# Strassen's seven products for the up-projections of two feed-forward layers

## The chip, the core and the metric

One core of a Trainium2 chip runs the whole program. The metric is the device time of one execution in microseconds (us). The engines named here are TensorE (PE: matmuls, with its weight loads as PEld), VectorE (DVE), ScalarE (ACT) and SyncE (SP, which issues DMAs). PSUM has eight banks of 512 float32 columns on 128 partitions; a matmul writes into one of them.

## What is computed

Two transformer blocks, one after the other, on one sequence of 1024 tokens with 1024 channels, all in float32: a mixer (state space, Fourier and attention branches in the first block; a gated recurrence and its neighbours in the second), then a feed-forward layer (FFN), each with norms and a residual. The FFNs are what the change is about:

```
up = dwconv3(h @ w_up, conv_w, conv_b)          # FFN 1, w_up: 1024 x 2*2816, width-3 convolution over tokens
gate, val = split(up, 2)
y = (gelu(gate) * val) @ w_down                 # w_down: 2816 x 1024

hid = square(relu(u @ w_up))                    # FFN 2, w_up: 1024 x 4096
m = hid @ w_down                                # w_down: 4096 x 1024
```

## The kernel before

Every float32 product is made of three passes: an operand x is split into `hi`, its cast to a shorter type (ScalarE), and `lo = x - hi` (VectorE), and the product is hi·hi + lo·hi + hi·lo (`mm3`, L144 to L156; `split`, L171). A weight block is 128 x 1024; `Weights._prep` (L121) loads it (512 KB, SP queue), casts it (L130) and subtracts (L131), one block ahead of its use. There are three buffers each for `whi` and `wlo`.

The up-projection puts hidden channels on the output's partitions: a block of 128 hidden channels is 8 channel steps x 3 passes x 2 halves of the tokens = 48 matmuls of 512 columns into two banks (`lin`, L159). FFN 1 makes a gate block and a value block (`ps_g`, `ps_v`; L418 on), convolves each out of PSUM (`conv`, L401: one ScalarE instruction, L406, and two VectorE instructions, L409 and L410), applies gelu (L427), multiplies (L429) and splits the result into `ghi` and `glo`. FFN 2 makes one block, relu on ScalarE (L449), its square on VectorE (L450), and splits it. FFN 1 has 22 such steps, FFN 2 has 32. The first blocks after a boundary are made by parts of the tokens (`halves`, L371), since the activations (`acth`, `actl`) come in by parts.

The down-projection puts tokens on the partitions: `rows_group` (L347) takes two hidden blocks, and for each of eight row tiles runs 2 x 3 x 2 matmuls into `ps_row` and adds the result to Y in SBUF (`rows_sum`, L329, VectorE L335; the first group is copied by ScalarE, L333). `ffn` (L384) goes by groups of two hidden blocks: up-projection of group G, then down-projection of group G - 1; the last group takes four blocks and runs beside the boundary (norm, residual, transposes, next activations). So up- and down-projection alternate through the whole FFN, and the hidden blocks stay in SBUF.

Each engine works through its instructions in a fixed order, which a scheduler lays down when the program is built.

## Time and profile before

| | |
|---|---|
| median of 3 runs | 2741.04 us (2740.24 to 2744.2) |
| span of the profiled execution, first to last instruction | 2737.2 us |
| PE busy | 2675.8 us (98%), 12572 matmul records |
| PEld busy | 2195.7 us (80%) |
| VectorE busy | 1449.3 us (53%) |
| ScalarE busy | 885.0 us (32%) |
| mean granted TensorE clock | 0.995 of 2.4 GHz |

The time of a run lies some 4 us above the span. Mixer 1 takes 0 to 455, FFN 1 480 to 1147, the boundary behind it to 1215, mixer 2 to 2020, FFN 2 2055 to 2695, and the rest is its last group and the output. Matmuls overlap in their records (0.39 us each, one started every 0.23 us), so the pace of PE is read from starts.

### The profile page before, as it was taken

What the parts mean: (1) busy time and instruction counts of PE and PEld (TensorE: products, weight loads), DVE (VectorE), ACT (ScalarE), POOL (GpSimd) and SP (SyncE); (2) the same over time, 40 slices, a digit from 0 to 9 for tenths busy, and PEclk for the clock granted to TensorE, in tenths of its full rate; (3) what the DMA queues carried; (4) which work ended last, traced back from release to release, by engine and by line L of the source; (5) the groups of instructions that cost most, each with busy time, mean ns of one, the idle gap of its engine ahead of it and who ended that gap; (6) DMA issues with size and microseconds to landing.
All of it is one profiled execution on the core that took longest, in us unless ns stands there. A gap on an engine that the chain in (4) does not pass through costs nothing.

```text
span 2737.2 us, 30502 instructions
## 1 busy us (share of the span) xinstructions
PE 2675.8 (98%) x12572; PEld 2195.7 (80%) x12572; DVE 1449.3 (53%) x2428; ACT 885.0 (32%) x1335; POOL 0.2 (0%) x4
## 2 busy tenths in 40 slices
...
GB/s 257 86 71 146 164 57 179 54 47 46 54 47 46 47 47 46 71 130 39 39 39 34 54 45 40 54 46 54 77 155 56 52 47 47 47 54 39 58 51 108
DMA packets 65484, 193.62 MB, mean 71 GB/s; under 512 B 10305, under 2 KB 19905, under 8 KB 65346
## 3 DMA queue, kind: packets, MB, share of 16 engines
...
## 4 chain that ended last, share of the span: by engine, by line
PE 88%; DVE 7%; ACT 2%; DMA 1%; issue 1%; SPq 0%; ACTq 0%; DVEq 0%
PE ps_row L322 8%; PE ps_row L324 8%; PE ps_row L326 8%; PE ps_z L154 7%; PE ps_z L156 7%; PE ps_z L152 7%; PE ps_u L152 4%; PE ps_u L156 4%; PE ps_u L154 4%; PE ps_g L152 3%; PE ps_v L152 3%; PE ps_g L154 3%; PE ps_v L154 3%; PE ps_g L156 3%; PE ps_v L156 3%; PE ps_bo L152 1%
## 5 line engine op out<-in xcount | busy, mean ns | idle before, releaser
L131 DVE TENSOR_TENSOR wlo<-wraw,whi 128x1024 fp32r<-128x1024 f32 x208 | 254.3, 1223 | 871.7 <-ACT whi L130 871.5
L130 ACT CAST whi<-wraw 128x1024 fp32r<-128x1024 f32 x208 | 218.8, 1053 | 1219.3 <-PE ps_row L326 330.4
L335 DVE TENSOR_TENSOR y<-y,ps_row 128x512 f32<-128x512 f32 x398 | 256.2, 681 | 151.1 <-PE ps_row L326 151.1
L152 PE MATMUL ps_z<-acth,whi 128*128 128x512 f32 x960 | 302.3, 396 | 0.2 <-ACT z L1046 0.2
L154 PE MATMUL ps_z<-actl,whi 128*128 128x512 f32 x960 | 300.1, 392 | 1.9 <-DVE actl L173 1.9
L156 PE MATMUL ps_z<-acth,wlo 128*128 128x512 f32 x960 | 298.1, 391 | 0.0
L324 PE MATMUL ps_row<-wlo,ghi 128*128 128x512 f32 x792 | 245.4, 389 | 0.0
L322 PE MATMUL ps_row<-whi,ghi 128*128 128x512 f32 x792 | 245.3, 389 | 0.0
L326 PE MATMUL ps_row<-whi,glo 128*128 128x512 f32 x792 | 244.1, 389 | 0.0
L154 PEld LDWEIGHTS ps_z<-actl,whi 128*128 128x128 f32 x960 | 179.9, 188 | 40.2 <-DVE actl L173 2.4
L156 PEld LDWEIGHTS ps_z<-acth,wlo 128*128 128x128 f32 x960 | 179.9, 188 | 37.3 <-issue 0.2
L152 PEld LDWEIGHTS ps_z<-acth,whi 128*128 128x128 f32 x960 | 178.4, 188 | 39.0 <-issue 1.7
L322 PEld LDWEIGHTS ps_row<-whi,ghi 128*128 128x128 f32 x792 | 148.7, 188 | 31.1
L326 PEld LDWEIGHTS ps_row<-whi,glo 128*128 128x128 f32 x792 | 148.7, 188 | 31.0
L324 PEld LDWEIGHTS ps_row<-wlo,ghi 128*128 128x128 f32 x792 | 148.6, 188 | 30.7
L152 PE MATMUL ps_u<-acth,whi 128*128 128x512 f32 x480 | 147.8, 389 | 0.0
L154 PE MATMUL ps_u<-actl,whi 128*128 128x512 f32 x480 | 147.8, 389 | 0.0
L156 PE MATMUL ps_u<-acth,wlo 128*128 128x512 f32 x480 | 147.8, 389 | 0.0
L156 PEld LDWEIGHTS ps_u<-acth,wlo 128*128 128x128 f32 x480 | 90.1, 188 | 18.7
L154 PEld LDWEIGHTS ps_u<-actl,whi 128*128 128x128 f32 x480 | 90.1, 188 | 18.7
L152 PEld LDWEIGHTS ps_u<-acth,whi 128*128 128x128 f32 x480 | 90.1, 188 | 18.6
L154 PE MATMUL ps_g<-actl,whi 128*128 128x512 f32 x336 | 103.5, 389 | 0.0
...
## 6 DMA issues: line engine op xcount, KB each, us to landing
wraw<-in_W SPq DMA_DIRECT2D x216, 512.0 KB, 3.2
scr<-in_wa SPq DMA_DIRECT2D x32, 512.0 KB, 3.8
xr<-y SPq DMA_DIRECT2D x24, 512.0 KB, 2.9
xl<-xr SPq DMA_DIRECT2D x24, 512.0 KB, 4.4
wa<-in_wa SPq DMA_DIRECT2D x16, 512.0 KB, 4.8
x<-in_x SPq DMA_DIRECT2D x8, 512.0 KB, 7.4
xl<-in_x SPq DMA_DIRECT2D x8, 512.0 KB, 5.0
out<-y SPq DMA_DIRECT2D x7, 512.0 KB, 2.9
```

The source lines that it names most:

```text
L130: nc.scalar.copy(hi, r)
L131: nc.vector.tensor_tensor(out=lo, in0=r, in1=rr(hi), op=ALU.subtract)
L152: nc.tensor.matmul(ps(h), lhsT=wh, rhs=xh[:, cut(h)], start=a, stop=False)
L154: nc.tensor.matmul(ps(h), lhsT=wh, rhs=xl[:, cut(h)], start=False, stop=False)
L156: nc.tensor.matmul(ps(h), lhsT=wl, rhs=xh[:, cut(h)], start=False, stop=z)
L322: nc.tensor.matmul(ps[c], lhsT=xh, rhs=wh[:, S2H[c]], start=a, stop=False)
L324: nc.tensor.matmul(ps[c], lhsT=xh, rhs=wl[:, S2H[c]], start=False, stop=False)
L326: nc.tensor.matmul(ps[c], lhsT=xl, rhs=wh[:, S2H[c]], start=False, stop=z)
L335: k.V.tensor_tensor(out=o, in0=o, in1=ps[c], op=ALU.add)
```

## The change

Both up-projections are computed on pairs of column blocks. The activations are seen as a 2 x 2 matrix of quarters (tokens 0 to 511 and 512 to 1023, channels 0 to 511 and 512 to 1023: a11, a12, a21, a22), a pair of weight blocks as a 2 x 2 matrix of channel halves by blocks. Strassen's scheme (in Winograd's form) needs seven products of quarters in place of eight: `strassen` runs seven products of 4 channel steps x 3 passes = 12 matmuls, each product into one bank, 84 matmuls for a pair in place of 96. Two banks take two products each. Sums of activations (s1 to s4, `act_sums`) are made once per FFN, sums of weights (`_pair`) once per pair, and the four output quarters are put together by five VectorE additions and two ScalarE copies per pair. Pairs alternate between four single-bank tiles (`ps_q`) and two two-bank tiles (`ps_p`).

FFN 1 has 2 hidden steps in the old way and 10 gate pairs and 10 value pairs; FFN 2 has 4 blocks in the old way and 14 pairs. The hidden blocks go to DRAM (`hd`, a 512 KB DMA each, issued by ScalarE), and the down-projection follows as a phase of its own (`Down`): it loads each hidden block and its weight block, splits both, and goes by groups of 2, 2, 2, 4, 4, 4, 4 blocks in FFN 1 and 2, 2 and seven times 4 in FFN 2. FFN 2's square is a ScalarE instruction now. The convolution reads SBUF (`y`) in place of PSUM.

```diff
+    def _pair(self, b):
+        V = self.k.nc.vector
+        r0, r1 = self._raw(b), self._raw(b + 1, self.k.wx)
+        a, z = slice(0, 4), slice(4, 8)
+        u, t = (self.k.wx.tile([P, KT, P], F32, tag="ws", bufs=2, name=n) for n in ("ws_u", "ws_t"))
+        tt = lambda o, x, y: V.tensor_tensor(out=o, in0=x, in1=y, op=ALU.subtract)
+        X = self._split(r0, self._turn())
+        tt(t[:, a], r1[:, a], r0[:, a])
+        tt(u[:, a], r1[:, z], t[:, a])
+        tt(u[:, z], r1[:, z], r1[:, a])
+        U = self._split(u, self._turn())
+        tt(t[:, z], r0[:, z], u[:, a])
+        T_ = self._split(t, self._turn())
+        hi, lo = (self.k.wx.tile([P, 4, P], F32R, tag=n, bufs=2, name=n) for n in ("wvh", "wvl"))
+        split(self.k, hi, lo, r1[:, z])
...
+def strassen(k, act, w, banks, y0, y1, mid=None):
...
+    def product(ps, a, b, first):
+        ah, al = act.q[a]
+        bh, bl = w[b]
+        mm = lambda x, y, start=False, stop=False: nc.tensor.matmul(ps, lhsT=x, rhs=y, start=start, stop=stop, skip_group_check=True)
+        for i in range(4):
+            xh, xl = ah[i // 2][:, i % 2], al[i // 2][:, i % 2]
+            mm(bh[:, i], xh, start=first and i == 0)
+            mm(bh[:, i], xl)
+            mm(bl[:, i], xh, stop=i == 3)
+
+    add = lambda o, x, y: V.tensor_tensor(out=o, in0=x, in1=y, op=ALU.add)
+    product(pa, "a11", "b11", True)
+    nc.scalar.copy(y0[:, l], pa)
+    product(pb, "s2", "t2", True)
+    add(y1[:, l], y0[:, l], pb)
+    product(pc, "s3", "t3", True)
+    add(y1[:, h], y1[:, l], pc)
+    product(pd, "s1", "t1", True)
+    if mid:
+        mid()
+    product(pa, "a12", "b21", False)
+    product(pc, "a22", "t4", False)
+    add(y1[:, h], y1[:, h], pd)
+    add(y0[:, h], y1[:, l], pc)
+    product(pd, "s4", "b22", False)
+    add(y1[:, l], y1[:, l], pd)
+    return pa
...
+def act_sums(k, act, place, tmp):
...
+        a21, s = whole("a21"), whole("a22")
+        tt(s, s, a21, Ad)
+        split(k, act.q["s1"][0][j], act.q["s1"][1][j], s)
...
+def four_banks(k, odd):
+    if odd:
+        ps = [k.pmm.tile([P, T], F32, tag="pmm", name="ps_p") for _ in range(2)]
+        return [p[:, o] for p in ps for o in S2H]
+    return [k.psm.tile([P, H], F32, tag="psm", name="ps_q") for _ in range(4)]
...
+            for tt in range(8):
+                ps = (row_halves if last or tt % 2 == 0 else row_pair)(k)
+                rows(k, parts, lhs, tt, ps)
+                rows_sum(k, ps, Y[tt], G == 0)
+                if last:
+                    bnd.row(Y, tt)
+                elif tt % 2 == 1 and len(self.got) < self.sizes[G + 1]:
+                    self.prep(G + 1)
...
+            head(tile_, sums, out)
+            finish(sums)
+            tail(tile_, out, dn.first)
...
+    def tail(spare, out, mid):
+        for f in range(2, 22, 2):
+            cs = []
+            for b in (0, 22):
+                ys = [spare(f"y{j}") for j in range(2)]
+                p = strassen(k, act, w.next(), four_banks(k, b), *ys, mid if f == 20 and b else None)
+                nc.scalar.copy(ys[0][:, S2H[0]], p)
+                for j in range(2):
+                    c = spare("cg" if b == 0 else "cv")
+                    conv([ys[j]], c, b + f + j)
...
-            V.tensor_tensor(out=r, in0=r, in1=r, op=ALU.mult)
...
+            nc.scalar.activation(r, r, AF.Square)
```

How the order moves is shown at three places. In the names, `ws_t`, `ws_u` are sums of weights, `wraw` a weight block as loaded, `wlo`, `wvl` their lo parts, `xa` sums of activations, `s0` to `s11` and `s4h`, `s4l` the split sums of activations.

First, VectorE at the start of FFN 1. Before, it makes the lo parts of the second and third blocks' weights (the first of them for `ps_g`, the other for `ps_v`) between convolutions:

```order
L131 TENSOR_TENSOR wlo_4331<-wraw_4328,whi_4330 128x1024 [waits DMAHW1_49,PE_49,Activation_49]
L409 SCALAR_TENSOR_TENSOR cg<-ps_half,pcol,cg 128x511 [waits Activation_49]
L410 SCALAR_TENSOR_TENSOR cg<-ps_half,pcol,cg 128x511 [waits DVE_49]
L414 SCALAR_TENSOR_TENSOR cg<-ps_half,pcol,cg 128x1
L413 SCALAR_TENSOR_TENSOR cg<-ps_half,pcol,cg 128x1 [waits DVE_49]
L131 TENSOR_TENSOR wlo_4385<-wraw_4382,whi_4384 128x1024 [waits DMAHW2_49,PE_49,Activation_49]
L409 SCALAR_TENSOR_TENSOR cv<-ps_half,pcol,cv 128x511 [waits Activation_49]
L410 SCALAR_TENSOR_TENSOR cv<-ps_half,pcol,cv 128x511 [waits DVE_49]
L414 SCALAR_TENSOR_TENSOR cv<-ps_half,pcol,cv 128x1
L413 SCALAR_TENSOR_TENSOR cv<-ps_half,pcol,cv 128x1 [waits DVE_49]
L429 TENSOR_TENSOR cg<-cg,cv 128x1024 [waits DVE_49,Activation_49]
```

Now, after eight sums of activations (the first half of the channel steps), three splits of them and the same convolutions, the lo part for `ps_v` stands first here, and the first pair's weights and the other half of the sums follow:

```order
L324 TENSOR_TENSOR wlo<-wraw_4367,whi 128x1024 [waits DMAHW1_49]
L642 TENSOR_TENSOR cg<-cg,cv 128x1024 [waits DVE_49,Activation_49]
L324 TENSOR_TENSOR wlo<-wraw_4421,whi 128x1024 [waits DMAHW2_49]
L155 TENSOR_TENSOR ws_t<-wraw_4423,wraw_4421 128x512 [waits DMAHW3_49]
L155 TENSOR_TENSOR ws_u<-wraw_4423 128x512
L155 TENSOR_TENSOR ws_u<-wraw_4423,ws_t 128x512 [waits DVE_49]
L324 TENSOR_TENSOR wvl<-wraw_4423,wvh 128x512
L155 TENSOR_TENSOR ws_t<-wraw_4421,ws_u 128x512 [waits DVE_49]
L295 TENSOR_TENSOR xa_4495<-a21h,a21l 128x1024
L324 TENSOR_TENSOR wlo<-ws_u,whi 128x1024 [waits PE_49,Activation_49]
L295 TENSOR_TENSOR xa_4497<-a22h,a22l 128x1024
L295 TENSOR_TENSOR xa_4502<-a11h,a11l 128x1024
```

What moved: the lo part for `ps_v` stands behind the sums, and the lo part of the first pair's U (`ws_u`), which waits for matmuls of `ps_g`, has sums of activations queued ahead of it and behind it.

Second, VectorE in the middle of FFN 1. Before, one hidden block's share (beside it stand the `ps_row` additions):

```order
L131 TENSOR_TENSOR wlo_5355<-wraw_5352,whi_5354 128x1024 [waits DMAHW5_49,PE_49,Activation_49]
L409 SCALAR_TENSOR_TENSOR cg<-ps_g,pcol,cg 128x1023 [waits Activation_49]
L410 SCALAR_TENSOR_TENSOR cg<-ps_g,pcol,cg 128x1023 [waits DVE_49]
L131 TENSOR_TENSOR wlo_5409<-wraw_5406,whi_5408 128x1024 [waits DMAHW6_49,PE_49,Activation_49]
L409 SCALAR_TENSOR_TENSOR cv<-ps_v,pcol,cv 128x1023 [waits Activation_49]
L410 SCALAR_TENSOR_TENSOR cv<-ps_v,pcol,cv 128x1023 [waits DVE_49]
L429 TENSOR_TENSOR cg<-cg,cv 128x1024 [waits DVE_49]
L173 TENSOR_TENSOR glo<-cg,ghi 128x1024 [waits Activation_49]
```

Now, part of one gate pair (`ps_q`):

```order
L324 TENSOR_TENSOR wlo<-ws_u,whi 128x1024 [waits PE_49,Activation_49]
L229 TENSOR_TENSOR y_5596<-y_5596,ps_q 128x512 [waits DVE_49]
L155 TENSOR_TENSOR ws_t<-wraw_5732,wraw_5730 128x512 [waits DMAHW7_49,DMAHW6_49,DVE_49]
L229 TENSOR_TENSOR y_5596<-y_5596,ps_q 128x512 [waits DVE_49,PE_49]
L324 TENSOR_TENSOR wlo<-ws_t,whi 128x1024 [waits PE_49,Activation_49]
L155 TENSOR_TENSOR ws_u<-wraw_5732,ws_t 128x512 [waits DVE_49]
L155 TENSOR_TENSOR ws_u<-wraw_5732 128x512
L229 TENSOR_TENSOR y_5595<-y_5596,ps_q 128x512 [waits PE_49]
L324 TENSOR_TENSOR wlo<-wraw_5730,whi 128x1024 [waits Activation_49]
L155 TENSOR_TENSOR ws_t<-wraw_5730,ws_u 128x512 [waits DVE_49]
L229 TENSOR_TENSOR y_5596<-y_5596,ps_q 128x512 [waits DVE_49,PE_49]
L629 SCALAR_TENSOR_TENSOR cg<-y_5595,pcol,cg 128x1023 [waits Activation_49]
```

What moved: the additions that put a pair together stand between the splits and sums of the next pair's weights, in one queue, several of them behind instructions that wait for PE or ScalarE.

Third, PE at the end of a value pair (`ps_p`). Before, a finished block is followed by the row tiles:

```order
L154 MATMUL ps_v<-actl_3542,whi_5742 128x512 x2
L156 MATMUL ps_v<-acth_3534,wlo_5743 128x512 x2
L322 MATMUL ps_row<-whi_5796,ghi 128x512 x2
L324 MATMUL ps_row<-wlo_5797,ghi 128x512 x2
L326 MATMUL ps_row<-whi_5796,glo 128x512 x2
```

Now, the sixth product's last two matmuls, ten matmuls of the next pair's first product, the seventh product (which goes on in the bank that VectorE has to have read), and the rest of that first product:

```order
L222 MATMUL ps_p_6023<-a22l_3542,whi_5881 128x512
L222 MATMUL ps_p_6023<-a22h_3540,wlo_5882 128x512
L222 MATMUL ps_q_6155<-a11h_3527,whi_6002 128x512
L222 MATMUL ps_q_6155<-a11l_3529,whi_6002 128x512
...
L222 MATMUL ps_q_6155<-a11h_3528,whi_6002 128x512
L222 MATMUL ps_p_6023<-s4h_4523,wvh_5885 128x512 [waits DVE_49]
L222 MATMUL ps_p_6023<-s4l_4525,wvh_5885 128x512
L222 MATMUL ps_p_6023<-s4h_4523,wvl_5886 128x512
...
L222 MATMUL ps_p_6023<-s4h_4524,wvl_5886 128x512
L222 MATMUL ps_q_6155<-a11l_3530,whi_6002 128x512
L222 MATMUL ps_q_6156<-s4_4319,whi_6009 128x512 [waits Activation_49]
```

What moved: ten matmuls of the next pair are laid between the sixth product and the seventh, which waits for VectorE.

## Rows read from the trace of the kernel before

**Rows 1.** Busy time by stretch: each engine's us (instructions), then PEclk, DMA share, GB/s

```profile
core 0: us, PE busy (x) PEld busy (x) DVE busy (x) ACT busy (x) POOL busy (x), PEclk, DMA share, GB/s
0.00:455.00 455.00, 422.25 (x2252) 328.57 (x2252) 337.56 (x811) 245.05 (x543) 0.20 (x4) 0.99 0.40 135
480.00:1147.00 667.00, 667.00 (x2965) 553.12 (x2964) 315.99 (x331) 171.61 (x171) 0.00 (x0) 1.00 0.15 49
1147.00:1215.00 68.00, 61.22 (x313) 50.64 (x312) 53.69 (x134) 47.77 (x87) 0.00 (x0) 0.95 0.41 140
2055.00:2695.00 640.00, 640.00 (x2825) 530.14 (x2824) 275.00 (x332) 130.50 (x136) 0.00 (x0) 1.00 0.14 48
```

**Rows 2.** Waits of PE over the span: us in total, times, longest

```profile
PE ps_half L152 <- DVE st L189: 6.4, 1, 6.4
...
PE ps_hk L1384 <- DVE hkd L1381: 2.8, 4, 0.9
```

**Rows 3.** Timeline of PE in FFN 1, matmuls by turns into two banks: start us, us

```profile
616.11 0.62 PE L322 MATMUL ps_row<-whi,ghi 128*128 128x512 f32 x2
...
617.47 0.39 PE L322 MATMUL ps_row<-whi,ghi 128*128 128x512 f32 x1
```

**Rows 4.** Timeline of PE ahead of FFN 2, matmuls in a row into one bank

```profile
2031.47 0.40 PE L152 MATMUL ps_half<-acth,whi 128*128 128x512 f32 x1
...
2033.29 0.39 PE L156 MATMUL ps_half<-acth,wlo 128*128 128x512 f32 x1
```

**Rows 5.** Timeline of PE in mixer 2, in groups of six into one bank

```profile
1750.77 0.40 PE L152 MATMUL ps_bo<-byh,whi 128*128 128x512 f32 x1
...
1752.41 0.40 PE L154 MATMUL ps_bo<-byl,whi 128*128 128x512 f32 x1
```

**Rows 6.** Timeline of PE after the longest idle time ahead of FFN 2

```profile
2027.01 0.69 PE L240 MATMUL ps_tr<-ident,z 128*128 128x128 f32 x2 [5.69 <-ACT z L232]
...
2028.36 0.63 PE L156 MATMUL ps_half<-acth,wlo 128*128 128x512 f32 x1
2028.78 0.63 PE L152 MATMUL ps_half<-acth,whi 128*128 128x512 f32 x1
```

**Rows 7.** VectorE groups in FFN 1 (480 to 1147): busy us, mean ns, idle before

```profile
L335 DVE TENSOR_TENSOR y<-y,ps_row 128x512 f32<-128x512 f32 x128 | 82.6, 681 | 39.2 <-PE ps_row L326 39.2
L131 DVE TENSOR_TENSOR wlo<-wraw,whi 128x1024 fp32r<-128x1024 f32 x61 | 74.6, 1223 | 285.3 <-ACT whi L130 285.3
...
L410 DVE SCALAR_TENSOR_TENSOR cg<-ps_g,pcol,cg 128x1023 f32<-128x1023 f32 x21 | 26.9, 1283 | 0.7
...
L409 DVE SCALAR_TENSOR_TENSOR cg<-ps_half,pcol,cg 128x511 f32<-128x511 f32 x2 | 1.5, 746 | 0.8 <-ACT cg L406 0.8
```

**Rows 8.** VectorE, two SBUF operands of 512 columns (mixer 1)

```profile
L173 DVE TENSOR_TENSOR actl<-u,acth 128x512 fp32r<-128x512 f32 x16 | 10.3, 684 | 0.9 <-ACT acth L172 0.9
```

**Rows 9.** ScalarE groups in FFN 1 (480 to 1147)

```profile
L130 ACT CAST whi<-wraw 128x1024 fp32r<-128x1024 f32 x62 | 65.4, 1055 | 334.2 <-PE ps_g L154 129.0 <-PE ps_row L326 105.3 <-PE ps_v L154 97.7
L406 ACT ACTIVATE cg<-ps_g,pcol 128x1024 f32<-128x1024 f32 x21 | 25.3, 1203 | 0.0
```

**Rows 10.** VectorE group of FFN 2 (2055 to 2695) that the change moves

```profile
L450 DVE TENSOR_TENSOR rl<-rl 128x1024 f32<-128x1024 f32 x31 | 37.8, 1218 | 6.6 <-ACT rl L449 6.6
```

**Rows 11.** Start of FFN 1: timeline of VectorE

```profile
479.64 0.43 DVE L173 TENSOR_TENSOR actl<-u,acth 128x256 fp32r<-128x256 f32 x1 [0.73 <-ACT acth L172]
...
497.26 1.23 DVE L131 TENSOR_TENSOR wlo<-wraw,whi 128x1024 fp32r<-128x1024 f32 x1 [3.96 <-ACT whi L130]
```

**Rows 12.** Start of FFN 1: timeline of PE

```profile
485.52 0.63 PE L152 MATMUL ps_g<-acth,whi 128*128 128x512 f32 x2
```

**Rows 13.** Start of FFN 2: timeline of VectorE

```profile
2043.98 1.51 DVE L254 SCALAR_TENSOR_TENSOR actl<-ps_tr,pcol,acth 128x256 fp32r<-128x256 f32 x3 [0.34 <-ACT acth L253]
```

**Rows 14.** Start of FFN 2: timeline of PE

```profile
2052.23 0.63 PE L152 MATMUL ps_u<-acth,whi 128*128 128x512 f32 x2
```

**Rows 15.** DMA issues of the page: KB each, median us to landing

```profile
wraw<-in_W SPq DMA_DIRECT2D x216, 512.0 KB, 3.2
```

More of the change, by code (lines that the diff above doesn't have):

```diff
@@ L132, in _prep @@
[L132 to L136 removed]
+            split(self.k, hi, lo, r)
+            self.parts[u] = (hi, lo)
+        else:
+            self.parts[u] = self._split(self._raw(b))
+    def _pair(self, b):
[13 more added lines that the diff above has]
+        split(self.k, hi, lo, r1[:, z])
+        half = lambda x, o: (x[0][:, o], x[1][:, o])
+        return dict(b11=half(X, a), b21=half(X, z), b22=(hi, lo), t1=half(T_, a), t2=half(U, a), t3=half(U, z), t4=half(T_, z))
@@ L141, in next, with take @@
         return out if n > 1 else out[0]
+    def take(self, room=None):
+        if self.loaded == self.pos:
+            kind, b = self.units[self.pos]
+            r = self._raw(b)
+            if room:
+                hi, lo = (room(F32R).rearrange("p (m c) -> p m c", c=P) for _ in range(2))
+                split(self.k, hi, lo, r)
+                self.parts[self.pos] = (hi, lo)
+            else:
+                self.parts[self.pos] = self._split(r)
+            self.loaded += 1
+        self.pos += 1
+        return self.parts.pop(self.pos - 1)
 def mm3(nc, ps, rhs, halves, first=True, last=True):
@@ new lines, with __init__, prep, first @@
+class Down:
+    def __init__(self, k, w, hd, sizes, place):
+        self.k, self.w, self.hd, self.sizes, self.place = k, w, hd, sizes, place
+        self.done, self.got = 0, []
+    def prep(self, G):
+        k, w = self.k, self.w
+        j = len(self.got)
+        inside = (len(self.sizes) - 1 - G) % 2 == 1
+        act = lambda i, c: k.ap.tile([P, T], F32R, tag=f"a{c}{i}", name="dn" + c)
+        at = iter("hl")
+        if inside:
+            part = w.take(lambda dt: act(4 + j, next(at)))
+            lhs = [act(j, c) for c in "hl"]
+        else:
+            part = w.take(None if j < 3 else lambda dt: self.place(2 + "hl".index(next(at)), [P, T], dt))
+            lhs = [self.place(4 + 2 * j + c, [P, T], F32R) for c in range(2)]
+        r = self.place(self.done % 2, [P, T], F32)
+        k.nc.sync.dma_start(out=r, in_=self.hd[self.done])
+        split(k, *lhs, r)
+        self.done += 1
+        self.got.append((part, lhs))
+    def first(self):
+        for _ in range(self.sizes[0]):
+            self.prep(0)
+    def run(self, pool, bnd):
+        k = self.k
+        Y = [pool.tile([P, T], F32, name=f"y{m}") for m in range(8)]
+        n = len(self.sizes)
+        for G in range(n):
+            last = G == n - 1
+            if last:
+                bnd.start()
+                if bnd.act is None:
+                    k.V = InOrder(k.tc, k.nc.vector)
+            parts, lhs = zip(*self.got)
+            self.got = []
+            for tt in range(8):
+                ps = (row_halves if last or tt % 2 == 0 else row_pair)(k)
+                rows(k, parts, lhs, tt, ps)
+                rows_sum(k, ps, Y[tt], G == 0)
+                if last:
+                    bnd.row(Y, tt)
+                elif tt % 2 == 1 and len(self.got) < self.sizes[G + 1]:
+                    self.prep(G + 1)
@@ L432, in ffn1, with hidden, head @@
-    ffn(k, w, 11, up, bnd)
+    def hidden(pg, pv, f, spare, out):
+        cg = spare("cg")
+        conv(pg, cg, f)
+        nc.scalar.activation(cg, cg, AF.Gelu_apprx_tanh)
+        cv = spare("cv")
+        conv(pv, cv, 22 + f)
+        V.tensor_tensor(out=cg, in0=cg, in1=cv, op=M)
+        out(f, cg)
+    def head(spare, sums, out):
+        pg, pv = halves(k, w, act)
+        next(sums)
+        hidden(pg, pv, 0, spare, out)
+        pg, pv = ([k.pmm.tile([P, T], F32, tag="pmm", name=n)] for n in ("ps_g", "ps_v"))
+        for p in (pg, pv):
+            lin(k, lambda h, p=p: p[0][:, S2H[h]], w.next(), act)
+        next(sums)
+        hidden(pg, pv, 1, spare, out)
```

204 lines of the change are left out of this document (131 added, 73 removed).

## The prediction

> **What bounds the kernel now.** I read the table by stretches first. In FFN 1 (480 to 1147) PE is busy for 667.00 of 667.00 us and in FFN 2 (2055 to 2695) for 640.00 of 640.00, with the granted clock at 1.00, while VectorE works 316.0 and 275.0 us there and ScalarE 171.6 and 130.5 [rows 1]. The view of waits says the same from the other side: PE's longest waits all stand at boundaries and in mixers, none in an FFN [rows 2]. So in both FFNs matmuls are the only bound; taking them out gives time one for one until VectorE or ScalarE is late, and only what makes PE wait is a cost. Then I read the pace of PE in the timeline, the VectorE and ScalarE groups for prices, and the order of the changed program for what stands in front of what.
>
> **What goes.** A pair took 96 matmuls of 512 columns and takes 84. With 20 pairs in FFN 1 and 14 in FFN 2, 34 x 12 = 408 matmuls go; the down-projection keeps its own. Six starts from 616.11 to 617.47 make 0.2267 us each [rows 3], so 408 x 0.2267 = **-92.5 us** (54.4 in FFN 1, 38.1 in FFN 2).
>
> **Pace of the new matmuls.** Two neighbours used to alternate between two banks; now twelve go into one. Two rows show one-bank runs. Ahead of FFN 2 eight starts from 2031.47 to 2033.29 are 0.2275 apart [rows 4], the old pace to a hundredth; in mixer 2 seven from 1750.77 to 1752.41 are 0.234 apart, inside the groups of six as well as between them, so a change of bank isn't what costs there [rows 5]. 34 x 84 = 2856 matmuls at the two paces cost 2 or 21 us. I take the first (runs longer than six, operands from the same activations) and +1; both ends stay in the range.
>
> **Prices on VectorE.** 1.223 us for 128 x 1024 from SBUF and 0.681 for 512 columns with one operand in PSUM [rows 7], 0.684 for 512 from SBUF [rows 8], 1.28 for a convolution half and 0.75 for one of 511 columns [rows 7]; that the convolution now reads SBUF I cost at nothing, since 512 columns are 0.68 either way. Casts on ScalarE are 1.055, the convolution's first step 1.20 [rows 9].
>
> **FFN 1, middle.** A gate pair and a value pair are 168 matmuls, 38.1 us. VectorE has 36 instructions in that time: 10 additions (6.8), 8 weight subtractions (5.5), 6 splits of 1024 (7.3), 2 of 512 (1.4), 8 convolution halves (10.2), 2 products (2.4): 33.7 us, about 34.5 with gaps, 91% against 47% before [rows 1]. ScalarE has some 17. The work fits, but in order. The tightest place is a `ps_p` pair: its seventh product waits for VectorE's reading of the fourth bank after the sixth, two additions of 0.68 and whatever is in hand (up to 1.28), 1.4 to 2.6 us; the ten matmuls that the order lays between are 2.27. The other: U and T get their lo parts only after a buffer is released by PE and a cast, 1.06 + 1.22 = 2.3, with a product (2.7) ahead of the use. So stalls are between nothing and one exposed chain of 2.3 in each of 20 pairs, 46 us. By these covers a miss is some tenths of a microsecond per pair: **+5**.
>
> **FFN 1, start.** Here VectorE is the bound. Before, the last activation lo part ends at 480.1, and little follows [rows 11]. Now 8 sums and 3 splits stand among the halves' convolutions ahead of the lo part for `ps_v`: 12 x 1.22 + 8 x 0.75 and small ones, 22.8 us from 478.6, so 501.4. PE starts `ps_g` at 485.52 [rows 12], ends it 48 x 0.2267 later at 496.4, and with the six matmuls that need no lo part it waits from 497.8: **3.6**. `ps_v` then ends at 511.4, and T's lo part, which waits for its release, holds the queue; 12.0 us of other work keep VectorE until 513.4 anyway. The 15 instructions to the last split of s4 are 18.6, so 532.0, and the next pair's first lo part 533.2. PE runs out of what it may do at 527 (58 matmuls after 511.4, 2.0 lost on parts of s1 to s3): **6.2** and **2.0**. Behind it U of the second pair, its third and its first addition are late by 2.0, 0.4 and 3.0: **5.4**. Together 17.2, I take **+18**; 10 if only the first and the third are felt, 30 if the convolutions also wait for ScalarE in this queue.
>
> **FFN 2, start.** The same without convolutions: 21.6 us of VectorE from 2045.4 [rows 13] put the fourth block's lo part at 2067.0; PE, which begins `ps_u` at 2052.23 [rows 14], wants it at 2064.0: 3.0, and the first pair's U 1.6 late: **+5** (0 to 12).
>
> **FFN 2, middle.** VectorE 10.5 and ScalarE some 9 of 19.0 us per pair; the square's 1.22 [rows 10] goes to ScalarE, which has room: **+1** (0 to 10).
>
> **Down-projection.** VectorE adds 144 results fewer (larger groups), 98 us at 0.681; none of it was awaited in the FFN, so it gives nothing. Splitting the hidden blocks only moves. Hidden blocks go out and in, 54 x 512 KB each way; a group of four loads eight tiles, 8 x 3.2 = 26 us even one after the other [rows 15], beside 192 matmuls, 43.5 us: hidden. Without that cover a group would begin some 3 us late. The fourth block of a group is prepared only after the last row tile: two additions, two splits, 4.0 us, needed 4.1 after it. About ten such joints: **+3** (0 to 10). Twice the phase begins right after the last pair, with its first two blocks loaded and split behind that pair's work: **+4** (0 to 12). That the last group has no row tiles begun early costs at most the 6.8 us that PE idles there now [rows 1]; I put it into these.
>
> **Clock.** After 5.69 us of idle time matmuls started 0.42 us apart, 1.2 GHz, for a few starts [rows 6]. The 6 us stall and the phase changes may do this: **+2** (0 to 8).
>
> The sum: -92.5 + 1 + 5 + 18 + 5 + 1 + 3 + 4 + 2 = -53.5. Against the profiled span of 2737.2, 2683.7; the median 2741.04 lies 3.8 above the span, so **2687.5**.
>
> **Rivals.**
>
> *PE hardly waits.* The covers of the order hold, VectorE's start is made up by work that PE has ready: only the first stall at FFN 1's start, 6 us of others, -82: 2659. For it: nearly everywhere a product of 2.7 us stands between a need and its use. Against it: the VectorE queue at 478 to 533, which is full by count. Chance 0.17.
>
> *The slow pace.* All 2856 at 0.234: 2687.5 + 20 = 2708. Chance 0.10.
>
> *FFN 1's middle is VectorE's.* At 91% a queue that also waits loses a microsecond or two in each of 20 pairs, 20 to 45 us in place of 5: 2703 to 2728. Chance 0.11.
>
> *Slower: the VectorE queue loses time in every pair.* An addition that PE waits for stands behind a lo part that itself waits for PE and ScalarE; if the seventh product and U's lo part each lie open, 2.3 + 1.3 us per pair, that is 34 x 3.6 = 122 in place of 6, and 2804. It decides from (92.5 - 33) / 34 = 1.75 us per pair on. For it: 20 of the 36 instructions of two pairs wait for PE or ScalarE. Against: the ten matmuls laid before the seventh product, and VectorE's 45% of free time in FFN 2. Chance 0.08. The Trainium skill, PSUM — Partial Sum Buffer, Engine vs sequencer instructions, says that VectorE's queue is strictly first in, first out; by that rule nothing overtakes a waiting lo part, which is what this rival needs. No row here shows it by itself.
>
> *The clock.* Short waits in every pair might bring the clock down: 0.42 in place of 0.227 for a tenth of the 2856 matmuls is 55 us, no change in sum. In mixer 1, where PE idles for 33 of 455 us in many pieces, the granted clock is 0.99 [rows 1], so I give it 0.02. The Trainium skill, TensorE: Matmul & The Clock Gate, A second HAM failure mode: psum-queue depth-cycling, tells of a kernel that went through its banks in turn, idled for moments between groups and swung between the two clocks; the mixer's row doesn't agree with that here.
>
> That the change doesn't do what it says I exclude: the order lists 84 matmuls for a pair.
>
> **How the numbers follow.** My sum has 0.52, with its own range of 2670 to 2703; the others as given. What a measurement can tell from no change is about 0.2%, 5.5 us. All cases but the last two are faster, 0.90, less 0.02 for the upper end of FFN 1's middle, which may come within 0.2%; of the last two's 0.10, 0.01 may come out within and 0.09 slower: faster 0.88, within 0.03, slower 0.09. The range from 2650 to 2730 leaves out the slower rivals and a little below.
>
> **What would show it.** In the profile after: 408 matmuls fewer, the FFN stretches with PE close to full; waits of PE for VectorE's lo parts and sums gathered within 60 us of FFN 1's start, some 18 us, and fewer at FFN 2's; in the middle of FFN 1 VectorE above 85% and PE's waits under 1 us each; starts 0.227 apart in `ps_q`; the down phase with waits of some tenths at its joints. I am wrong if PE waits in each pair for more than half a microsecond, if the starts inside a product are 0.23 or more apart, or if the clock is below 0.98.

## The result and the profile after

| | before | after |
|---|---|---|
| median (range, runs) | 2741.14 us (2740.24 to 2744.2, 4) | 2667.57 us (2666.55 to 2668.49, 4) |
| ratio, 95% interval | | 0.973 (0.9716 to 0.9744) |
| span of the profiled execution | 2737.2 us | 2664.8 us |
| PE busy, matmul records | 2675.8 us, 12572 | 2594.8 us, 12164 |
| VectorE, ScalarE busy | 1449.3, 885.0 us | 1625.9, 1022.2 us |
| mean granted clock | 0.995 | 0.993 |

The changed kernel is 73.6 us faster; forecast were 53.5. The records are 408 fewer, as counted. Where the time went is read from first matmuls of the stretches, here those of after on PE (start us, us):

```profile
485.37 0.40 PE L204 MATMUL ps_g<-a11h,whi 128*128 128x512 f32 x1
...
1183.46 0.63 PE L204 MATMUL ps_z<-acth,whi 128*128 128x512 f32 x2
...
2015.10 0.40 PE L204 MATMUL ps_u<-a11h,whi 128*128 128x512 f32 x1
```

| stretch | before | after | change | by fewer matmuls alone | left over |
|---|---|---|---|---|---|
| FFN 1 and what follows (first `ps_g` to mixer 2's first `ps_z`) | 735.8 | 698.1 | -37.7 | -54.4 | 16.7 |
| mixer 2 (to FFN 2's first `ps_u`) | 830.9 | 831.6 | +0.7 | 0 | 0.7 |
| FFN 2 (to the end of the span) | 685.0 | 649.7 | -35.3 | -38.1 | 2.8 |

Before, the same starts stood at 485.52 [rows 12], 1221.31 and 2052.23 [rows 14]; the second of them:

```profile
1221.31 0.40 PE L152 MATMUL ps_z<-acth,whi 128*128 128x512 f32 x1
```

The changes add up to -72.3, the difference of the spans to a tenth. So the question is the 19.5 us in FFN 1 and FFN 2 that the change costs, where the forecast put 39.

The table by stretches of after, to be laid beside [rows 1]: FFN 1's start, two pairs of its middle, the start of its down-projection, FFN 2's start, one pair of its middle, its down-projection:

```profile
core 0: us, PE busy (x) PEld busy (x) DVE busy (x) ACT busy (x) POOL busy (x), PEclk, DMA share, GB/s
485.37:583.60 98.23, 91.70 (x391) 74.19 (x389) 91.24 (x105) 44.18 (x48) 0.00 (x0) 0.97 0.23 81
583.60:621.90 38.30, 38.30 (x168) 31.09 (x167) 32.43 (x38) 17.21 (x20) 0.00 (x0) 1.00 0.23 83
902.65:1064.00 161.35, 158.76 (x693) 130.79 (x692) 89.42 (x108) 45.58 (x54) 0.00 (x0) 0.99 0.40 133
2015.10:2036.90 21.80, 21.80 (x99) 18.03 (x98) 21.80 (x21) 12.47 (x14) 0.00 (x0) 1.00 0.25 97
2065.00:2084.00 19.00, 19.00 (x84) 15.63 (x84) 9.82 (x13) 8.23 (x11) 0.00 (x0) 1.00 0.31 112
2306.60:2620.00 313.40, 312.79 (x1379) 258.42 (x1379) 140.84 (x178) 70.30 (x80) 0.00 (x0) 1.00 0.30 103
```

PE idles 6.5 us in FFN 1's start, where VectorE is busy for 91.24 of 98.23 us, and nowhere in a pair of the middle. FFN 2's start has VectorE busy for 21.80 of 21.80 us and PE as well: nobody waits for it. The main waits of PE that are new or have grown, against [rows 2] (us in total, times, longest):

```profile
PE ps_p L222 <- DVE wlo L324: 5.6, 1, 5.6
...
PE ps_row L473 <- ACT y L484: 3.2, 2, 2.6
PE ps_row L473 <- DVE y L486: 2.5, 2, 1.3
```

One wait for a lo part, and a few at the joints of the down-projection. PE's timeline around the first shows what it costs beyond itself:

```profile
521.09 0.39 PE L222 MATMUL ps_p<-a11l,whi 128*128 128x512 f32 x1
527.05 0.80 PE L222 MATMUL ps_p<-a11h,wlo 128*128 128x512 f32 x1 [5.57 <-DVE wlo L324]
...
528.50 0.63 PE L222 MATMUL ps_p<-a11h,wlo 128*128 128x512 f32 x1
528.93 0.63 PE L222 MATMUL ps_p<-a11h,whi 128*128 128x512 f32 x1
```

From 527.05 to 532.7 starts are 0.43 apart (528.50 to 528.93), 1.2 GHz, as in [rows 6]. The time by which starts lie further apart than 0.227 adds up, over FFN 1's pairs, to 12.1 us: 5.7 in this wait, 2.8 at the low clock behind it, 1.0 in one wait for an addition at 547.1, and the rest in small steps, most of them one or two starts 0.34 apart in a `ps_p` pair. FFN 1's down-projection has 4.6, of which 2.6 are the wait at 914.70 and 1.8 the low clock behind it (granted 0.5 from 914.9 to 918.3). FFN 2 has 1.25 in its pairs and 1.15 in its down-projection. Apart from that the pace is the old one [rows 3]; twelve in a row into one bank, in `ps_q` of FFN 2:

```profile
2045.73 0.61 PE L222 MATMUL ps_q<-s,whi 128*128 128x512 f32 x2
2046.18 0.39 PE L222 MATMUL ps_q<-s,wlo 128*128 128x512 f32 x1
2046.41 0.61 PE L222 MATMUL ps_q<-s,whi 128*128 128x512 f32 x2
2046.86 0.39 PE L222 MATMUL ps_q<-s,wlo 128*128 128x512 f32 x1
```

Five starts (x2 is two matmuls) in 1.13 us: 0.226 each. VectorE's timeline in FFN 1's start says why it was ready sooner than forecast:

```profile
476.98 1.23 DVE L295 TENSOR_TENSOR xa<-a21h,a21l 128x1024 f32<-128x1024 f32 x1
...
496.25 1.21 DVE L324 TENSOR_TENSOR wlo<-wraw,whi 128x1024 fp32r<-128x1024 f32 x1
497.38 1.21 DVE L642 TENSOR_TENSOR cg<-cg,cv 128x1024 f32<-128x1024 f32 x1
498.52 1.21 DVE L324 TENSOR_TENSOR wlo<-wraw,whi 128x1024 fp32r<-128x1024 f32 x1
499.65 0.68 DVE L155 TENSOR_TENSOR ws_t<-wraw,wraw 128x512 f32<-128x512 f32 x1
500.26 0.67 DVE L155 TENSOR_TENSOR ws_u<-wraw 128x512 f32<-128x512 f32 x1
...
525.78 1.22 DVE L324 TENSOR_TENSOR wlo<-wraw,whi 128x1024 fp32r<-128x1024 f32 x1
```

After one of 1.21 the next starts 1.13 later, after one of 0.68 the next 0.61 later: records overlap by 0.07 or 0.08, and a full queue goes by starts. The forecast went by records of [rows 7, 8], in the middle with gaps added; and the first sum, at 476.98, was over before the 478.6 from which it counted. The lo part for `ps_v` ended at 497.46 (forecast 501.4, wanted at 497.8), the one at 525.78 at 527.00 (forecast 533.2).

### The profile page after: what moved, and what is told of

The parts are those of the page before. It is cut to its first block, busy times and chain, and to the rows that moved or that the text cites. A ratio compares the mean times of both kernels' runs of the same rounds, so it can differ in the third digit from the quotient of the medians.

```text
span 2664.8 us, 30674 instructions
## 1 busy us (share of the span) xinstructions
PE 2594.8 (97%) x12164; PEld 2118.7 (80%) x12164; DVE 1625.9 (61%) x2674; ACT 1022.2 (38%) x1519; POOL 0.2 (0%) x4
## 4 chain that ended last, share of the span: by engine, by line
PE 86%; DVE 8%; ACT 2%; DMA 2%; issue 1%; SPq 0%; ACTq 0%; DVEq 0%
PE ps_q L222 11%; PE ps_p L222 11%; PE ps_z L206 7%; PE ps_z L204 7%; PE ps_z L208 7%; PE ps_row L473 5%; PE ps_row L475 5%; PE ps_row L477 5%; PE ps_rows L473 4%; PE ps_rows L477 4%; PE ps_rows L475 4%; PE ps_bo L204 1%; PE ps_bo L206 1%; PE ps_bo L208 1%; PE ps_o L1151 1%; PE ps_s L1126 1%
## 5 line engine op out<-in xcount | busy, mean ns | idle before, releaser
L324 DVE TENSOR_TENSOR wlo<-wraw,whi 128x1024 fp32r<-128x1024 f32 x148 | 180.2, 1220 | 349.1 <-ACT whi L323 348.8
L486 DVE TENSOR_TENSOR y<-y,ps_row 128x512 f32<-128x512 f32 x160 | 103.3, 681 | 135.6 <-PE ps_row L477 135.6
L486 DVE TENSOR_TENSOR y<-y,ps_rows 128x512 f32<-128x512 f32 x112 | 71.8, 682 | 111.0 <-PE ps_rows L477 110.9
L222 PE MATMUL ps_p<-s,whi 128*128 128x512 f32 x408 | 128.8, 397 | 0.2
L222 PE MATMUL ps_q<-s,whi 128*128 128x512 f32 x408 | 125.8, 389 | 0.0
L222 PEld LDWEIGHTS ps_p<-s,whi 128*128 128x128 f32 x408 | 75.1, 189 | 21.7 <-DVE y L229 4.4
L222 PEld LDWEIGHTS ps_q<-s,whi 128*128 128x128 f32 x408 | 76.6, 188 | 16.1 <-DVE s L324 0.2
L473 PE MATMUL ps_row<-whi,s 128*128 128x512 f32 x240 | 76.1, 396 | 4.5 <-ACT y L484 3.2
L222 PE MATMUL ps_p<-s,wlo 128*128 128x512 f32 x204 | 79.7, 390 | 0.0
L222 PE MATMUL ps_q<-s,wlo 128*128 128x512 f32 x204 | 79.2, 389 | 0.0
```

The costliest lines, as they stand in the source:

```text
L222: mm = lambda x, y, start=False, stop=False: nc.tensor.matmul(ps, lhsT=x, rhs=y, start=start, stop=stop, skip_group_check=True)
L324: k.nc.vector.tensor_tensor(out=lo, in0=x, in1=rr(hi), op=ALU.subtract)
L473: nc.tensor.matmul(ps[c], lhsT=xh, rhs=wh[:, S2H[c]], start=a, stop=False)
L486: k.V.tensor_tensor(out=o, in0=o, in1=ps[c], op=ALU.add)
```

## The experiments

My theory after the result: the 408 matmuls give the whole gain, the new phases nothing; what is left over is VectorE's in-order queue, at FFN 1's start alone; two sets of banks keep its lateness from PE in the middle. Rivals: part of the gain is the phases'; the middle is near VectorE's bound; the wait sits in some other place than the sums. Every kernel was timed beside the kernel before on its chip. The first `ps_g` lies between 485.37 and 492.25 us in the traces, though the versions don't differ ahead of it, so two that are a few microseconds apart are told better from the length of FFN 1 and FFN 2 in their traces (after: 698.1 and 649.7) than from medians.

**Phases without the products** (`plain_up`): all hidden blocks in the old way, hidden blocks in DRAM and down-projection as after.

```diff
-        pg, pv = halves(k, w, act); ...
-        hidden(pg, pv, 1, spare, out)
+        for f in range(1, 22):
+            pg, pv = ([k.pmm.tile([P, T], F32, tag="pmm", name=n)] for n in ("ps_g", "ps_v"))
...
-    def tail(spare, out, mid):
+    tail = None
```

> Both FFNs keep the new phases (hidden blocks to DRAM, down-projection after them, its group sizes), but every hidden block is made in the old way, 48 matmuls each, with no sums. Theory A (the whole gain is the 408 matmuls, and the separate phases give nothing): the 408 come back at 0.2267, +92.5, and the waits among the products (some 14 us in the trace of the changed kernel: 12.1 in FFN 1, 1.3 in FFN 2, the rest small) go: 2667.6 + 92.5 - 14 = 2746 us, between 2740 and 2752, and so no faster than the kernel before (2741). Theory B (part of the gain is from the phases themselves: 144 additions fewer, weights and hidden blocks loaded far ahead): 2725 us or less.

2743.09 us, ratio 0.9996 (0.9987 to 1.0005). FFN 1 takes 735.4 and FFN 2 684.9, the 735.8 and 685.0 of before. The phases alone give nothing and cost nothing; the gain is the products'.

**One set of banks** (`one_bank_set_p`: all pairs in two two-bank tiles; `one_bank_set_q`: all in four one-bank tiles).

```diff
 def four_banks(k, odd):
-    if odd:
+    if True:      # one_bank_set_p; in one_bank_set_q: if False
```

> All pairs take two two-bank tiles (ps_p), so a pair's third and fourth products write into a tile that the pair before has only just ended in, and every read of one bank holds up both. Theory A (PE goes on because ten matmuls of the next pair lie ahead of the seventh product; VectorE's queue has a sixth of its time free): the ten matmuls are still possible, in the tile that ends first; what is new is a wait of the third product for the last addition, 0.7 plus what VectorE has in hand, behind two products: 0.3 to 1.0 us for each of 34 pairs, +10 to +35, 2678 to 2703 us. Rival (the order of VectorE's queue decides, not the banks): no change, within 5 us of 2667.6.

> All pairs take four one-bank tiles (ps_q): the dependences of a product are those of its own bank. Theory A: in the trace of the changed kernel each ps_p pair has one or two starts 0.34 apart in place of 0.227, and one ps_p pair at the start of FFN 1 waits 1.0 for an addition; these go, some 3 us, but the next pair's first product has to wait for ScalarE's copy out of the first bank, which is done two products before: 2664 to 2668 us. Rival (alternation of two sets is needed): each pair loses half a microsecond or more, 2685 us or more.

The first: 2736.06 us, 0.9973 (0.9963 to 0.9982), 68.5 us over after; the gain is almost gone, and my 10 to 35 were too few. The second: 2666.35, 0.9721 (0.9706 to 0.9735), the time of after. Two pairs of FFN 1's middle in the first, then of the second:

```profile
667.50:710.80 43.30, 39.55 (x170) 31.04 (x168) 32.21 (x37) 16.58 (x18) 0.00 (x0) 1.00 0.22 73
```

```profile
700.00:738.10 38.10, 38.10 (x170) 31.55 (x169) 31.36 (x36) 16.61 (x19) 0.00 (x0) 1.00 0.24 84
```

VectorE does the same work in both, 32.2 and 31.4 us, yet the first needs 43.3 us for 168 matmuls. Its PE and its VectorE at one joint between pairs:

```profile
617.15 0.39 PE L222 MATMUL ps_p<-a11h,wlo 128*128 128x512 f32 x1
618.90 0.73 PE L222 MATMUL ps_p<-s,whi 128*128 128x512 f32 x2 [1.36 <-DVE y L229]
...
625.49 0.50 PE L222 MATMUL ps_p<-a12h,whi 128*128 128x512 f32 x1 [0.85 <-DVE y L229]
```

```profile
615.65 1.28 DVE L629 SCALAR_TENSOR_TENSOR cv<-y,pcol,cv 128x1023 f32<-128x1023 f32 x1
616.96 1.28 DVE L630 SCALAR_TENSOR_TENSOR cv<-y,pcol,cv 128x1023 f32<-128x1023 f32 x1
618.17 0.68 DVE L229 TENSOR_TENSOR y<-y,ps_p 128x512 f32<-128x512 f32 x1
```

The seventh product of a pair ends in the second tile. The next pair's second product goes into the same tile only two matmuls later, and a tile is free as a whole: it waits for the last addition, and that stands behind two convolution halves (2.5 us) that are not urgent. (Second in PE's order; by what it waits for, it is the code's third.) With four one-bank tiles the order has 36 matmuls, 8.2 us, between a pair's last product and the next into its bank; with two sets in turn the next pair writes elsewhere. Either is enough. With neither, the pairs lose 69.2 us, where those of after lose 13.4: 2.0 in each of 34 pairs, 2.6 in FFN 1's middle (43.3 for 38.1 in two pairs), about 1 in FFN 2 (14.5 in 14 pairs), where VectorE is half free. A further wait stands ahead of the first pair, whose tile a convolution still reads as `ps_g`:

```profile
PE ps_p L222 <- DVE cg L630: 9.0, 1, 9.0
```

The 2.0 are over the slower rival's point of 1.75, and the kernel is still not slower than before only because the rest costs some 18 us, less than the 33 counted there. In FFN 1's middle (541.4 to 974.9) the granted clock stays 1.00 through these waits; it was 0.5 from 517.5 to 527.7, around the end of the wait of 9.0, and for 3.4 us each behind waits of 3.5 us at 537.1 and 2.8 us at 2108.2.

**Where FFN 1's start waits.** `head4` makes two more hidden steps in the old way (24 more matmuls, 5.4 us); `s4late` puts the splitting of the last sum (s4), which only the seventh product needs, inside the first pair.

```diff
-        for f in range(2, 22, 2):
+        for f in range(4, 22, 2):      # head4; hidden steps 1 to 3 in the old way
```

```diff
-            finish(sums)
-            tail(tile_, out, dn.first)
+            tail(tile_, out, dn.first, lambda: finish(sums))
...
+                p = strassen(..., mid if f == 20 and b else s4 if f == 2 and not b else None)
```

> FFN 1 makes four hidden steps (eight blocks) in the old way ahead of the first pair in place of two: 24 matmuls more, +5.4 us. Theory A (the 5.7 us wait at 521, the 2.4 us of half clock behind it and the 1 us for an addition come from VectorE's backlog, which 21.8 us of old-way blocks with little work for VectorE let it catch up on): -9 + 5.4, 2663 to 2666 us. Rival (the wait is for the loads of the first pairs' weights or a release of their buffers, whatever VectorE has to do): the wait stays, 2672 to 2674 us.

> The split of s4 is emitted inside the first pair of each FFN (behind its fourth product) in place of ahead of it, so that two lo parts of 1024 columns stand behind the second pair's first lo part on VectorE. Theory A (PE's wait of 5.7 us at 521 is VectorE's backlog): that lo part comes 2.3 us earlier, the wait is 3.4, and less of the half clock follows: -2 to -5, 2663 to 2666 us. Rival (what VectorE is spared there is waited for at the seventh product or at the additions a few us later, since its queue is full until about 560): 2667 to 2668 us, with the wait moved.

`head4`: 2667.24, 0.9722 (0.9707 to 0.9736). What its pairs lose sinks from 12.1 to 2.1 us, more than the added matmuls cost, and FFN 1 takes 695.0 us, 3.1 less than in after, where theory A had 3.6. The medians, 0.3 apart, don't show it: in this trace the first `ps_g` came at 490.32, 4.9 later than in after. It is not more because a wait opens ahead of the added work:

```profile
515.19 0.47 PE L204 MATMUL ps_g<-a11h,whi 128*128 128x512 f32 x1 [2.45 <-DVE cg L630]
```

`s4late`: 2668.35, 0.9729 (0.9715 to 0.9743), FFN 1 698.2, no gain; the rival's, the wait moves. The one of 5.6 has become several of 0.9 to 2.5 (starts), two of them:

```profile
527.96 0.51 PE L222 MATMUL ps_p<-a11h,wlo 128*128 128x512 f32 x1 [2.12 <-DVE wlo L324]
...
532.04 0.73 PE L222 MATMUL ps_p<-s,whi 128*128 128x512 f32 x2 [1.47 <-ACT whi L323]
```

So the start is short of VectorE work done, not of one instruction in the wrong place.

**VectorE's room in the middle** (`vec6`): one weight subtraction is made seven times, six more of 512 columns per pair.

```diff
-        tt(u[:, z], r1[:, z], r1[:, a])
+        for _ in range(7):
+            tt(u[:, z], r1[:, z], r1[:, a])
```

> The changed kernel with the subtraction for the second half of U made seven times over for each pair (same result): 6 more VectorE instructions of 512 columns per pair, 12 in the time of two. Prices in dispute: by busy times (0.68) they are 8.2 us per two pairs, and with the 33.7 of the prediction's sum VectorE would need 41.9 of 38.3 us: +36 us in the middle of FFN 1, +10 at its start, 2710 us or more. By the starts in the trace of the changed kernel (0.60 apart for 512 columns, 1.13 for 1024) they are 7.2, beside 30.5: 37.7 of 38.3, just not the bound; some 1 us lost per two pairs to order, 10, and 7 to 10 at the start: 2680 to 2695 us. FFN 2 (14 of 19 us) loses under 4 either way.

2718.37 us, 0.9911 (0.9897 to 0.9924): in the first band (2710 or more), which went by busy times, and above the second, which went by starts. By the total the busy times win, but the trace doesn't bear their reason out. FFN 1's pairs lose 64.0 us in place of 12.1, FFN 2's 2.8. Two pairs of FFN 1 take 41.2 to 45.1 us, and VectorE isn't full; its subtractions start 0.60 apart:

```profile
684.00:728.50 44.50, 39.26 (x170) 31.27 (x169) 41.76 (x54) 17.52 (x20) 0.00 (x0) 1.00 0.23 83
```

```profile
724.75 0.68 DVE L155 TENSOR_TENSOR ws_t<-wraw,ws_u 128x512 f32<-128x512 f32 x1
725.35 0.68 DVE L155 TENSOR_TENSOR ws_u<-wraw 128x512 f32<-128x512 f32 x1
```

VectorE, ScalarE and PE of one such period (start us, us; idle before in brackets):

```profile
737.66 1.23 DVE L325 TENSOR_TENSOR wlo<-ws_u,whi 128x1024 fp32r<-128x1024 f32 x1 [5.69 <-ACT whi L324]
```

```profile
736.58 1.05 ACT L324 CAST whi<-ws_u 128x1024 fp32r<-128x1024 f32 x1 [10.02 <-PE ps_p L223]
```

```profile
729.62 0.79 PE L223 MATMUL ps_p<-a12h,whi 128*128 128x512 f32 x1 [3.98 <-DVE y L230]
730.21 0.63 PE L223 MATMUL ps_p<-a12l,whi 128*128 128x512 f32 x1
730.64 0.63 PE L223 MATMUL ps_p<-a12h,wlo 128*128 128x512 f32 x1
```

VectorE is so late that PE waits 4.0 us for an addition; then PE needs its time to release a weight buffer, ScalarE casts, and VectorE, whose next in line is that lo part, stands idle for 5.7 with later work behind it. An in-order queue that feeds PE and waits for PE loses time on both sides before it is full, though not long before; by starts VectorE's work here is 37.7 of 38.3 us. Some 10 of the 64 us are low clock: behind each wait like this one the starts are 0.43 apart (730.21 to 730.64), and the clock is granted at 0.5 for 3.4 us. The Trainium skill, PSUM — Partial Sum Buffer, Engine vs sequencer instructions, says that VectorE's queue is strictly first in, first out; these rows agree.

**Combining the two findings**: `q_s4late` (one-bank tiles and late s4), `q_late2` (also hidden step 1's convolution behind the first gate pair), `q_s4late_gp` (`q_s4late` with four sums of s4 on GpSimd).

```diff
-        hidden(pg, pv, 1, spare, out)
+        return lambda: hidden(pg, pv, 1, spare, out)
...
             for b in (0, 22):
+                if f == 2 and b:
+                    rest()
```

```diff
-        tt(a, rr(act.q["a12"][0][j]), rr(act.q["a12"][1][j]), Ad)
-        tt(a, a, s, Su)
+        G.tensor_tensor(out=a, in0=rr(act.q["a12"][0][j]), in1=rr(act.q["a12"][1][j]), op=Ad)
+        G.tensor_tensor(out=a, in0=a, in1=s, op=Su)
```

> One set of one-bank tiles for all pairs, and the split of s4 late. The run with one-bank tiles alone has no gaps in the middle but one wait of 11.2 us at 521 for an addition that stands behind the second pair's U. Theory A: two lo parts fewer ahead of it, 2.3 us: the wait is 8.9, 2663 to 2665 us. Rival: the backlog is waited out anyway, 2666 us.

> As q_s4late (one set of one-bank tiles, s4 split late), and the convolution of the second old-way hidden step in FFN 1, four VectorE instructions and a product, is emitted behind the first gate pair: its PSUM tiles are free for that, since no pair uses two-bank tiles. Theory A (VectorE's backlog, and room for it later, 17% of its time in the middle): 5 x 1.2 us fewer stand ahead of the awaited addition, so the wait of 8.9 us falls to about 3, and nothing comes back in the middle: 2656 to 2660 us. Rival (the backlog is waited out wherever it is put, as when s4 alone went late): 2662 to 2664 us.

> As the run before, and the four instructions for s4 (two sums, two differences of 1024 columns, per FFN) go from VectorE to GpSimd, which is idle. Theory A (VectorE's backlog at the start of FFN 1 is all that is left of the waits): 2 x 1.13 us fewer ahead of the awaited addition, another 2 behind it: the wait falls by 2 to 5 us more, 2659 to 2663 us. Rival (GpSimd takes much longer, no trace of before shows it at this, or slows VectorE beside it, since both read SBUF): the seventh product waits for s4, 2666 us or more.

`q_s4late`: 2663.8, 0.971 (0.9696 to 0.9723), FFN 1 694.6, with one wait of 8.9 between starts, as expected; its interval still touches that of after. `q_late2`: 2657.65, 0.9686 (0.9672 to 0.9701), clear of after: with less VectorE work ahead of the first pairs the wait halves and FFN 1's pairs lose 6.5.

```profile
528.53 0.50 PE L222 MATMUL ps_q<-a11h,whi 128*128 128x512 f32 x1 [3.60 <-DVE y L229]
```

`q_s4late_gp`: 2664.41, 0.9718 (0.97 to 0.9736), nothing gained. Its trace is of the slowest of four executions (2671.97 us; the others took 2660.61 to 2664.42). FFN 1's pairs lose 9.1, but FFN 2's 5.6 in place of 0, since one addition on GpSimd took 18.06 us and VectorE then waited for s4:

```profile
2018.91 18.06 POOL L314 TENSOR_TENSOR xa<-a12h,a12l 128x1024 f32<-128x1024 f32 x1 [1491.68 <-ACT s L324]
...
2039.39 2.40 POOL L314 TENSOR_TENSOR xa<-a12h,a12l 128x1024 f32<-128x1024 f32 x1
```

In FFN 1's start GpSimd needs 2.39 and 3.27 us, but there VectorE pays. Two splits that take 2.35 us at 487.26 of after took, beside GpSimd's 492.27 to 498.01:

```profile
492.62 6.47 DVE L325 TENSOR_TENSOR s<-xa,s 128x1024 fp32r<-128x1024 f32 x2
```

The next two, from 522.49, took 5.82. That is 7.6 us of VectorE lost for four instructions, 4.5 us by starts, taken off it: the rival's second reason.

**The two changes that I had costed at next to nothing**: `sq_vec` puts FFN 2's square back on VectorE, `groups2` goes by groups of two hidden blocks (a last one of four).

```diff
-                nc.scalar.activation(ys[j], ys[j], AF.Square)
+                nc.vector.tensor_tensor(out=ys[j], in0=ys[j], in1=ys[j], op=ALU.mult)
```

```diff
-    ffn(k, w, act, 22, head, tail, [2, 2, 2, 4, 4, 4, 4], bnd)
+    ffn(k, w, act, 22, head, tail, [2] * 9 + [4], bnd)
```

> The changed kernel with FFN 2's squares of the pairs on VectorE again: two instructions of 1024 columns more per pair, 2.3 us, beside 9.8 to 11.7 of 19.1. Theory A (in FFN 2 VectorE has room and nothing waits for a square): within 3 us of 2667.6. Rival (what stands in VectorE's queue is waited for even when it has room): 0.3 to 1.0 us per pair, 2672 to 2682 us.

> The down-projections by groups of two hidden blocks throughout, but for the last group of four: 16 + 12 results per token tile in place of 14 more of the larger ones, so 2 x 16 x 8 or so additions of 512 columns come back to VectorE (0.60 each), and PE ends a row tile every 2.7 us in place of 5.4. Theory A (additions are hidden beside PE, 1.2 of 2.7 us per row tile, and the larger groups gave nothing): within 4 us of 2667.6. Rival (in groups of two the splits of weights and hidden blocks, 4 x 1.13 in 21.8 us, and the additions hold each other up at every group's end): 1 us or more per group, 20 us, 2680 us or more.

2670.04, 0.9732 (0.971 to 0.9753), and 2666.72, 0.9717 (0.9701 to 0.9733): both intervals hold the 0.973 of after, and the trace of `sq_vec` has FFN 2 at 649.6 us, after's 649.7. (The groups of two bring back 9 x 16 = 144 additions, not the number that I wrote.) In `sq_vec` two pairs of FFN 2 have PE full and VectorE at 24.4 of 38.2 us:

```profile
2100.00:2138.20 38.20, 38.20 (x169) 31.29 (x168) 24.44 (x31) 12.80 (x17) 0.00 (x0) 1.00 0.31 110
```

**The joint to the down-projection** (`q_late3`). In after PE's wait at 914.70 is for ScalarE's copies of results, and ScalarE's timeline says what holds them (PE first, then ScalarE):

```profile
914.70 1.28 PE L473 MATMUL ps_row<-whi,s 128*128 128x512 f32 x2 [2.59 <-ACT y L484]
```

```profile
908.88 5.14 ACTq L598 DMA_DIRECT2D hd<-cg  x2
914.06 1.08 ACT L484 COPY y<-ps_row 128x512 f32<-128x512 f32 x2 [4.98 <-DVE cg L669]
```

The issue of the last two hidden blocks' writes stands in ScalarE's queue and waits there for VectorE's product, 5.14 us with the copies behind it. `q_late3` is `q_late2` with those two writes issued by SyncE.

```diff
-    out = lambda i, t: k.nc.scalar.dma_start(out=hd[i], in_=t)
+    out = lambda i, t: (k.nc.sync if i >= n - 2 else k.nc.scalar).dma_start(out=hd[i], in_=t)
```

> As q_late2, and the last two hidden blocks of each FFN go to DRAM from SyncE's queue in place of ScalarE's. Theory A (in the changed kernel PE waits 2.6 us at 912 because ScalarE's queue holds the down-projection's first copies behind two DMA issues, which wait for VectorE's last products): the wait at the start of FFN 1's down phase, 1.8 us in q_late2, goes, 2655 to 2658 us. Rival (the copies are late because VectorE's last products are what is waited for in any queue, or SyncE's loads are held up in turn): the wait stays or moves, 2657 to 2660 us.

2654.99, 0.968 (0.9665 to 0.9694): the fastest version, 12.6 us below after. The interval overlaps that of `q_late2`, so the last step is shown by the traces alone: FFN 1 takes 686.3 (`q_late2` 691.5, after 698.1), of which 681.4 are what before took less the matmuls that went. The wait at the start of FFN 1's down-projection, in `q_late2`

```profile
PE ps_row L473 <- ACT y L484: 1.8, 1, 1.8
```

is gone, and with it some 2 us of low clock behind it. Of the pairs' waits one is left among PE's longest, 3.7 us for an addition.

## Why the prediction was right, and what was mis-sized

The forecast of 2687.5 lay 19.9 us above the median, which is inside the range of 2650 to 2730 but just below the 2670 to 2703 that I gave my own sum. Its mechanism held, but for the middle of FFN 1; its costs were put at twice what was measured. By its steps:

- *What goes*, -92.5: 408 records fewer, and `plain_up` gives the phases no part in the gain. Right.
- *Pace*, +1: the median start is 0.227 apart in both FFNs' pairs; no trace of the 0.234 of [rows 5]. Right; the rival of the slow pace falls.
- *FFN 1, start*, +18: this is the mis-sized step. VectorE is the bound there, as said (30 of 30 us from 497 to 527), but the step counted 12 x 1.22 + 8 x 0.75 from busy records as if one began when the last had ended. `ps_v`'s lo part came 3.9 us before its forecast: 1.8 by the overlap (records of 20.5 us from 478.79 to 497.46, 18.7 us), 1.2 by the first sum that ran earlier, the rest because "small ones" stood for 2.2 us and were 1.2. From there to the next pair's first lo part 31.8 forecast us were 29.5. So the wait of 3.6 and the losses on parts of s1 to s3 vanish, and the third term stays, 5.7 for 6.2, with 1.0 for the 5.4 behind it: 6.7 in place of 17.2. (By the prediction's own numbers `ps_v` ends at 510.9, 42 matmuls after 501.4, and not at 511.4, which would make the third term about 1 us larger.)
- *FFN 2, start*, +5: 0. The fourth block's lo part ended 11.3 us after the first `ps_u` (2026.39), where 14.8 were forecast and PE wants it at 11.8: a cover of half a microsecond. Of the 3.5 us, 1.3 are the overlap (records of 19.4 us in the 18.1 from 2008.29); the rest is work that I had counted ahead of it and that did not stand there, 21.6 us for 19.4.
- *FFN 1, middle*, +5: about 2. VectorE is at 32.4 of 38.3, 85%, where 91% were forecast: the overlap again. The reason that I gave for the small loss was not the one that decides. I had the ten matmuls ahead of a pair's seventh product as its cover; `one_bank_set_p` keeps those ten (they stand at 611.9 to 613.9 of its trace) and loses 2.6 us per pair there all the same, most of it at the next pair's second product. What protects PE is where the next product into a tile stands.
- *FFN 2, middle*, +1: 1.25. `sq_vec` shows that moving the square was worth nothing by itself, to a tenth of a microsecond in FFN 2's length.
- *Down-projection and transitions*, +3 and +4: 5.75 in excess starts, 1.8 of them low clock. The size is right; the main piece, a DMA issue that holds ScalarE's copies, was not among those named. `groups2` shows that the number of groups doesn't matter.
- *Clock*, +2: 2.8 behind the wait of 5.6, and the 1.8 behind the wait at 914.70 that stand in the line above.

Forecast for all that speaks against the gain: 39. Measured: 19.5, of which the excess of starts named above makes 19.1.

Of the rivals, *PE hardly waits* (2659, with a first stall and 6 us of others) lies 8.6 us below the median, nearer than my own sum; its reason, that PE has other work ready, is not what happened, since VectorE stayed full and was merely quicker. *VectorE loses time in every pair* did not happen, but is real: `one_bank_set_p` pays its 2.0 us per pair. *The clock* fell in the FFNs of after only behind the two waits named above. Waits in every pair need not bring it down: two pairs of `one_bank_set_p`, with waits of 1.4 and 0.9 us, run at 1.00 (667.50 to 710.80). But they can: in `vec6` it is granted at 0.5 for 3.4 us behind each wait of 4.0 us (643.9, 729.2, 818.0 and 903.3), and once behind one of 2.2 (773.6). The Trainium skill, TensorE: Matmul & The Clock Gate, A second HAM failure mode: psum-queue depth-cycling, tells of such waits with a clock that swings; the rows of `vec6` agree, that of `one_bank_set_p` doesn't.

Open stays what the small steps of 0.34 in `ps_p` pairs are; they are gone with one-bank tiles (FFN 2's pairs in `one_bank_set_q` lose 0.0), so they belong to the two-bank tiles, but no run tells a wait from a slow start.
